# Inference step of a retention and HGRN2 mixer: gates by Silu, loads spaced out, two W_out operands split late

## The chip, the cores and the metric

The program runs on one core of one Trainium2 chip. The metric is the device time of one execution in microseconds. Five engines work side by side: TensorE (PE; its weight loads are listed as PEld), VectorE (DVE), ScalarE (ACT), GpSimd (POOL) and SyncE (SP), which here only issues DMA transfers. Each engine runs its own instructions strictly in its own order and waits at each for what that instruction needs. TensorE's results go to PSUM banks, from which ACT or DVE must copy them before the bank can be used again.

## The reference

One layer for 2048 prompt tokens and 8 decode tokens, width 1024, in fp32. After an RMS norm a projection makes eight groups of 512 columns; a retention branch (4 heads, rotary, fixed decay) and an HGRN2 branch (4 heads, learned forget gate) run over them; each branch's output is normed per head, multiplied by a SiLU gate, and both pass through one output projection.

```python
h = rmsnorm(x, norm_g)
rq, rk, rv, rg, hq, hf, hi, hgate = jnp.split((h @ w_in), 8, axis=-1)
...
o_ret = head_rmsnorm(o_ret, ret_g) * jax.nn.silu(rg)
...
kin = (1.0 - lbf) * jax.nn.sigmoid(-hf)
hq_act = jax.nn.silu(hq)
...
o_hg = head_rmsnorm(o_hg, hg_g) * jax.nn.silu(hgate)
o_cat = jnp.concatenate([o_ret, o_hg], axis=-1)
y = x + o_cat @ w_out
...
y_prompt = rmsnorm(hp, final_norm_g)
```

## The kernel before, in words

**Numbers and products.** A product in fp32 is made of three matmuls: each operand is split into a high part (rounded to the matmul's format, a copy on ACT) and a low part (the rest, a subtraction on DVE). `hi_lo` (L114 to L116) makes that pair; `split` puts it into the pool `wp`, three buffers each for `wh` and `wl`. `three` issues the matmuls (L339). Large products of 256 tokens by 1024 columns are done with seven half-size products instead of eight; this needs sums of the operand's quarters. On the weight side these sums are called T1 to T4, and the quarters used as they are B11, B12, B21, B22 (only B11, B21 and B22 in the seven).

**Stages.**
1. *Projection loop.* Sixteen chunks of 128 tokens form eight token pairs; three sets of weights run over them, so 24 passes, called pairs 0 to 23 here. Set 0 (pairs 0 to 7) makes the two values, set 1 (8 to 15) retention's q and its gate, set 2 (16 to 23) retention's k and HGRN2's gate. Pairs 0 and 1 are done by plain products; for the others `v_pair(i, after)` runs the seven products as steps 0 to 6, about 2.7 us of TensorE each; a product may go on adding in a bank that ACT has just copied (`keep`, L379). `after[n]` lists the side work issued behind step n: loads of the tokens two pairs on (`tok_load`), their scaling, splits and sums one pair on (`tok_ops`, `s_split`), and the sums of squares of the tokens (`stats`, L255 to L265), which give the RMS norm's scale `rs_all`. For pairs 2 to 5 of set 0, `stats(i + 2)` stands behind step 0: four loads of 256 KB into two buffers (`xn`, L262), four Squares on ACT (L263).
2. *The next set's weights.* While set m - 1 runs, pairs j = 3 to 6 of it load two rows of the next set's weights, add the decode tokens' products from them (`wg_decode`), and make the sums T1 to T4 (`w_sums`, L494 to L497), which go to DRAM (`wg_spool`, L520). In pair j = 7 `wg_decode_out` finishes the decode gate (L527 to L532), and `wg_fetch` (L548 to L563) loads the seven operands, 1 MB each: T's through POOL's queue as soon as TensorE has used the old ones, B's through SP. `wg_split` splits them.
3. *Outputs of a pair.* `emit` (L381 to L406) writes what a bank holds: values directly, q and k through the rotation `turn` (L341 to L364, with the table loaded by `rot_load`), gates through Sigmoid on ACT (L399) and a product on DVE (L400).
4. *Retention* rides in set 2 (`r_score`, `r_update`, `r_out`, `r_norm`, `r_turn`); its last chunk, 15, ends in the passage to the scan.
5. *Scan.* Eight units (two halves of the tokens, four HGRN2 heads): projections f and q of a unit run in segments (L980) on TensorE between the levels of the scan of the unit before (L1188 to L1238). Weights for the next projection are brought by `w_load_ahead`. On the side, `t_load_raw`, `t_sum`, `t_spool` and `t_store` make the sums T1 to T4 of W_out, split them and store both parts to DRAM.
6. *Out phase.* Four chunks by plain products (L1572), then six pairs, 2 to 7, by the seven products (`o_pair`); `y_out` norms a chunk and stores it. The last pair, chunks 14 and 15, ends the program.

**Order of the work.** TensorE's order is the order of the program text. The order on ACT, DVE, POOL and SP is laid out at compile time by a scheduler, by the order of the text and by what it reckons each instruction's time to be, with buffers handed out from each pool as they come free. `behind(f)` fixes that what f issues comes after the last instruction issued so far on DVE, ACT and SP; `queued` does so for the engines named. A pool that is opened where another was closed lies on the same storage, so its first use waits for the last use of the old tiles (`scan_pools`, L951 to L958, after `vctx` of the projection loop).

Of the kernel before, what the change touches and what calls it, by code (L numbers as in the profile page):

```python
# [10 lines left out]
F32 = mybir.dt.float32  # L11
# [30 lines left out]
def step_kernel(ctx, tc, a, out):  # L42
# [211 lines left out]

    def stats(i):  # L255
        p = V_ORDER[i]
        ms = sm.tile([P, 4], F32, tag="ms", name=f"ms{p}")
        for j in range(2):
            c = 2 * p + j
            for h in range(2):  # L260
                r = vq.tile([P, GW], F32, tag="xn", name=f"xn{c}{h}", bufs=2)
                sp.dma_start(r, a["x_prompt"][0, c * P : (c + 1) * P, h * GW : (h + 1) * GW])  # L262
                act.activation(r, r, AF.Square, accum_out=ms[:, 2 * h + j : 2 * h + j + 1])  # L263
        pool.tensor_tensor(ms[:, 0:2], ms[:, 0:2], ms[:, 2:4], op=ALU.add)
        rsqrt_mean(rs_all[:, 2 * p : 2 * p + 2], ms[:, 0:2], D, EPS)  # L265
# [106 lines left out]
    def v_pair(i, after):  # L372
# [8 lines left out]
        def emit(c, ty, ps, plus):  # L381
# [15 lines left out]
            if n_set and ty:  # L397
                sg = box[plus] if plus else o
                act.activation(sg, src, AF.Sigmoid)  # L399
                dve.tensor_tensor(o, src, sg, op=ALU.mult)  # L400
# [121 lines left out]
    def wg_decode_out(n):  # L522
# [5 lines left out]
        sg = vq.tile([NB, GW], F32, tag="rg", name=f"gds{n}")  # L528
        act.activation(sg, u, AF.Sigmoid)
        dve.tensor_tensor(u, u, sg, op=ALU.mult)  # L530
# [160 lines left out]
    tok_load(3)  # L691
    dve.tensor_tensor(lbd, lbraw[:, :, 0], lbraw[:, :, 1], op=ALU.subtract)
# [15 lines left out]
    def r_load(c, x):  # L708
        rb_of[c, x] = vq.tile([P, GW], F32, tag="r" + x, name=f"r{x}{c}")
# [75 lines left out]
    def r_steps(p):  # L785
# [22 lines left out]
        if p < N_V:  # L808
# [3 lines left out]
            put(4 + d, lambda: r_load(ca, "g"))  # L812
# [62 lines left out]
    for i in range(2, n_tok):  # L875
# [89 lines left out]
    def seg_steps(w, half, seg, name, evac):  # L965
# [21 lines left out]
    def w_load_ahead():  # L987
        while len(w_ready) < min(w_used[0] + AHEAD, len(want)):
            w_load()
# [281 lines left out]
    def collect(h, u):  # L1271
# [4 lines left out]
        (x, n): dr.tile([P, 2, 4, GW], F32, tag=f"t{x}{n}", name=f"t_dram{x}{n}") for x in "hl" for n in range(2)  # L1276
# [28 lines left out]
    def t_store(k, n):  # L1305
        for x, y in zip("hl", tspl[k, n]):
            sp.dma_start(t_dram[x, n][:, :, k], y.bitcast(F32).rearrange("p (a b) -> p a b", a=2))
# [60 lines left out]
    for k, at in enumerate((0.35, 1.35, 2.35, 4.35)):  # L1368
        steps = [t_load_raw] + [lambda k, n=n: t_sum(k, n) for n in range(4)]
        steps += [lambda k, n=n, f=f: f(k, n) for n in range(2) for f in (t_spool, t_store)]  # L1370
        for f, d in zip(steps, (0, 0.12, 0.18, 0.24, 0.3, 0.4, 0.48, 0.5, 0.58)):
# [154 lines left out]
    def t_load(n, pair):  # L1526
        for x, t in zip("hl", Top[n]):
            sp.dma_start(t.bitcast(F32), t_dram[x, pair[0]][:, pair[1]])

    def t2_load():  # L1530
        for x in "hl":
            t2.append([pools["vp"].tile([P, GW], F32R, tag="v", name=f"oT2{x}{n}") for n in range(4)])
            for n in range(4):
# [333 lines left out]
```

## Time and profile before

| | us |
|---|---|
| median of 3 runs | 1063.98 |
| lowest and highest | 1061.28 and 1064.03 |
| the profiled execution | 1064.47 |
| its span, first to last instruction | 1062.7 |
| its mean granted TensorE clock | 0.993 |

In the page's busy times an engine counts as busy while an instruction runs. A row of the order of time gives the start, the duration, the engine, the line, what is written and read, the count, and in brackets the idle time before it with what ended it. "issue" means that nothing in the profile was waited for. A row of the engine waits gives who waited, for what, the total in us, how often, and the longest. A row of the stretches gives the busy time of each engine, the granted clock of TensorE (1.00 is full speed), the share of the DMA engines that was busy, and GB/s. SPq, ACTq and POOLq mark the issue of a transfer.

### The profile page before, as it was taken

How to read it: one execution, taken by the hardware profiler on the slowest of the kernel's cores; microseconds unless marked ns; L12 is line 12 of the kernel's file. 1: busy time of each engine (PE TensorE's matmuls, PEld its weight loads, DVE VectorE, ACT ScalarE, POOL GpSimd, SP SyncE). 2: the span in 40 equal slices, each digit the busy share in tenths (PEclk: the TensorE clock that was granted, in tenths of full speed). 3: DMA queues.
4: the chain of work that ended last, by engine and by line, in shares of the span. 5: the costliest groups of instructions: out<-in, count | busy, mean ns of one | idle time of the engine just before them, and what ended most of it. 6: DMA issues, size and time to landing. Idle time of an engine off the chain costs nothing. (4 is left out here: it accounts for less than half of the span.)

```text
span 1062.7 us, 21303 instructions
## 1 busy us (share of the span) xinstructions
PE 1037.7 (98%) x8231; PEld 855.2 (80%) x8231; DVE 762.9 (72%) x1404; ACT 548.5 (52%) x1203; POOL 132.9 (13%) x232
## 2 busy tenths in 40 slices
PE   9999999899999999999999999999999999999997
PEld 7778778688787878888888879898778877888775
DVE  6885575887676796676676778777777687668785
ACT  7853343634434755455554656666555474523241
POOL 0410001000000101111111100111021112211122
PEclk9999999999999999999999999999999999999999
DMA  8688899757788855666875696664697366496652
GB/s 293 204 298 306 309 325 320 277 179 271 254 270 256 325 195 172 208 225 219 240 245 176 219 341 237 217 199 164 214 280 230 103 195 197 140 347 206 222 169 99
DMA packets 147462, 248.27 MB, mean 234 GB/s; under 512 B 10944, under 2 KB 78800, under 8 KB 147104
## 3 DMA queue, kind: packets, MB, share of 16 engines
q1 hardware_dynamic: 139632, 221.35, 62.8%
q0 software_dynamic: 7584, 25.29, 6.2%
q8 instruction: 65, 1.06, 0.4%
q14 instruction: 37, 0.30, 0.1%
q10 hardware_dynamic: 144, 0.26, 0.1%
HBM read 162.32 MB, written 84.54 MB: 232 GB/s over the span
## 5 line engine op out<-in xcount | busy, mean ns | idle before, releaser
L1168 ACT ACTIVATE kepth<-kh 128x1024 f32<-128x1024 f32 x24 | 25.4, 1059 | 69.6 <-DVE kh L1158 69.5
L980 PE MATMUL pjfh<-xh,w_h 128*128 128x512 f32 (+2 forms) x160 | 60.2, 376 | 0.0
L980 PE MATMUL pjqh<-xh,w_h 128*128 128x512 f32 (+2 forms) x160 | 60.1, 376 | 0.1
L980 PE MATMUL pjqh<-xh,w_l 128*128 128x512 f32 (+2 forms) x160 | 56.0, 350 | 0.0
L980 PE MATMUL pjfh<-xh,w_l 128*128 128x512 f32 (+2 forms) x160 | 56.0, 350 | 0.0
L980 PE MATMUL pjfh<-xl,w_h 128*128 128x512 f32 (+2 forms) x160 | 56.0, 350 | 0.0
L980 PE MATMUL pjqh<-xl,w_h 128*128 128x512 f32 (+2 forms) x160 | 55.8, 349 | 0.0
L1158 DVE TENSOR_TENSOR kh<-kh,fph 128x512 f32<-128x512 f32 x48 | 33.3, 694 | 20.2 <-PE plh L1188 14.2
L116 DVE TENSOR_TENSOR ab_l<-xr,ab_h 128x512 fp32r<-128x512 f32 (+1 forms) x40 | 37.5, 954 | 4.6 <-ACT ab_h L115 4.4
L752 ACT ACTIVATE obr<-por 128x128 f32<-128x128 f32 x64 | 16.8, 277 | 44.0 <-PE por L739 30.8
L115 ACT ACTIVATE ab_h<-xr 128x512 fp32r<-128x512 f32 (+1 forms) x40 | 32.3, 839 | 13.5 <-DVE xr L293 13.5
L762 DVE SCALAR_TENSOR_TENSOR obr<-por,omr,rg 128x128 f32<-128x128 f32 x64 | 18.0, 344 | 28.9 <-POOL omr L754 28.9
L293 DVE SCALAR_TENSOR_TENSOR xr<-xr,g_in,rb 128x256 f32<-128x256 f32 x64 | 26.7, 479 | 13.1 <-DMA xr<-in_x_t 11.2
L1090 DVE SCALAR_TENSOR_TENSOR obh<-poh,orsh,v 128x128 f32<-128x128 f32 x64 | 18.0, 344 | 25.2 <-POOL orsh L112 25.1
L980 PEld LDWEIGHTS pjqh<-xh,w_h 128*128 128x128 f32 x160 | 30.2, 189 | 5.3 <-issue 1.6
L980 PEld LDWEIGHTS pjfh<-xh,w_l 128*128 128x128 f32 x160 | 30.1, 188 | 4.2
L980 PEld LDWEIGHTS pjqh<-xh,w_l 128*128 128x128 f32 x160 | 30.1, 188 | 4.2
L980 PEld LDWEIGHTS pjfh<-xh,w_h 128*128 128x128 f32 x160 | 30.2, 189 | 3.8
L1161 DVE TENSOR_TENSOR qqh<-qqh,fph 128x512 f32<-128x512 f32 x48 | 32.9, 684 | 0.3 <-ACT kepth L1169 0.3
L980 PEld LDWEIGHTS pjfh<-xl,w_h 128*128 128x128 f32 x160 | 30.3, 189 | 2.7
L980 PEld LDWEIGHTS pjqh<-xl,w_h 128*128 128x128 f32 x160 | 30.2, 189 | 2.7
L1666 DVE SCALAR_TENSOR_TENSOR xro<-xro,yms,fg 128x1024 f32<-128x1024 f32 (+1 forms) x13 | 15.5, 1202 | 19.6 <-POOL yms L112 19.6
(1836 smaller groups left out, 3423.8 us busy)
## 6 DMA issues: line engine op xcount, KB each, us to landing
xr<-a_dram SPq DMA_DIRECT2D x24, 512.0 KB
S<-s_dram SPq DMA_DIRECT2D x24, 512.0 KB
xn<-in_x_prompt SPq DMA_DIRECT2D x32, 256.0 KB
xr<-in_x_t SPq DMA_DIRECT2D x16, 512.0 KB
a_dram<-xr SPq DMA_DIRECT2D x16, 512.0 KB
s_dram<-S SPq DMA_DIRECT2D x16, 512.0 KB
wgr<-in_w SPq DMA_DIRECT2D x16, 512.0 KB
xr<-a_dram SPq DMA_DIRECT2D x32, 256.0 KB
```

The lines of the kernel that those rows point to most:

```text
L115: act.activation(h, src, AF.Copy)
L116: dve.tensor_tensor(l, src, h.bitcast(F32), op=ALU.subtract)
L293: dve.scalar_tensor_tensor(r[:, k], r[:, k], g_in[:, kk : kk + 1], spread_to[i], op0=ALU.mult, op1=ALU.mult)
L752: act.activation(o[:, cc], po[:, h], AF.Square, scale=P ** -0.5, accum_out=ms[:, h : h + 1])
L762: dve.scalar_tensor_tensor(o[:, cc], po[:, h], ms[:, h : h + 1], rb_of[c, "g"][:, cc], op0=ALU.mult, op1=ALU.mult)
L980: pe.matmul(ps, ww[:, kk], x[:, k, b0 : b0 + n], start=(k == 0 and i == 0), stop=(k == KT - 1 and i == 2),)
L1090: dve.scalar_tensor_tensor(ob[g][:, j], po[:, j], rs[:, j : j + 1], gcol(4 * g + j), op0=ALU.mult, op1=ALU.mult)
L1158: dve.tensor_tensor(kv[:, :, 0, :], kv[:, :, 0, :], two[:, :, 1:2].to_broadcast([P, nb, b]), op=ALU.mult)
L1161: dve.tensor_tensor(qv[:, :, 1, :], qv[:, :, 1, :], two[:, :, 0:1].to_broadcast([P, nb, b]), op=ALU.mult)
L1168: act.activation(ss[:, 512:], k[:, :HALF], AF.Copy)
L1666: dve.scalar_tensor_tensor(xro[c][:, cc], xro[c][:, cc], ms[:, 0:1], fg[:, cc], op0=ALU.mult, op1=ALU.mult)
```

## The change

- **Gates.** In `emit` and `wg_decode_out` one Silu replaces Sigmoid and the product on DVE. A one-column Sigmoid is run in the passage to the scan.
- **Token squares.** `stats` is cut into load, sum and end. For pairs 2 to 5, the first half of the loads goes behind step 5 of the pair before (behind the prelude for pair 2), its Squares and the second half's loads behind step 1, the second Squares and the end behind step 4.
- **Rotation.** `rot_load(i + 1)` moves from step 6 to step 4, and the table has two buffers.
- **Gate weights.** Loading, decode products and sums run in pairs j = 2 to 5 of a set instead of 3 to 6; `decode_dg` and `decode_spread`, which scale the decode tokens, move from steps 3 and 5 of pair 2 to steps 0 and 2.
- **Scan weights.** `w_load_ahead` is called at part 2 of a segment too and does one load a call.
- **W_out.** Of the four sums, T1 and T4 are split in the scan as before; T2 and T3 are stored as they are (one store of 512 KB per k), loaded as they are and split in the out phase: T2 in four pieces during the plain chunks, T3 in two pieces behind steps 1 and 2 of pair 2.
- **Chunk 15 of retention.** Its gate is loaded into the pool `rawp`, and `r_norm` runs behind `scan_pools`. The gate of chunk 0 is loaded behind step 6.
- **Last pair.** Chunk 14's final scaling is issued after the last product has been added, ahead of chunk 15's, and is stored through SP instead of POOL.

```diff
+    def stats_load(i, j):
+        c = 2 * V_ORDER[i] + j
+        st[i, j] = [vq.tile([P, GW], F32, tag="xn", name=f"xn{c}{h}", bufs=2) for h in range(2)]
+        for h, r in enumerate(st[i, j]):
+            sp.dma_start(r, a["x_prompt"][0, c * P : (c + 1) * P, h * GW : (h + 1) * GW])
+
+    def stats_sum(i, j):
+        if not j:
+            st[i] = sm.tile([P, 4], F32, tag="ms", name=f"ms{V_ORDER[i]}")
+        for h, r in enumerate(st[i, j]):
+            act.activation(r, r, AF.Square, accum_out=st[i][:, 2 * h + j : 2 * h + j + 1])
...
-        rot[i] = vq.tile([P, 2, P], F32, tag="rot", name=f"rot{i}")
+        rot[i] = vq.tile([P, 2, P], F32, tag="rot", name=f"rot{i}", bufs=2)
...
-                sg = box[plus] if plus else o
-                act.activation(sg, src, AF.Sigmoid)
-                dve.tensor_tensor(o, src, sg, op=ALU.mult)
+                act.activation(o, src, AF.Silu)
...
-        sg = vq.tile([NB, GW], F32, tag="rg", name=f"gds{n}")
-        act.activation(sg, u, AF.Sigmoid)
-        dve.tensor_tensor(u, u, sg, op=ALU.mult)
+        act.activation(u, u, AF.Silu)
...
     tok_load(3)
+    stats_load(4, 0)
...
+        pl, tag = (rawp, "raw") if (c, x) == (2 * N_V - 1, "g") else (vq, "r" + x)
+        rb_of[c, x] = pl.tile([P, GW], F32, tag=tag, name=f"r{x}{c}")
...
-            put(4 + d, lambda: r_load(ca, "g"))
+            put(4 + d if p else 6, lambda: r_load(ca, "g"))
...
-            after[0] += [lambda i=i: stats(i + 2)]
+            after[1] += [lambda i=i: behind(lambda: stats_sum(i + 2, 0)), lambda i=i: stats_load(i + 2, 1)]
+            after[4] += [lambda i=i: behind(lambda: stats_sum(i + 2, 1)), lambda i=i: stats_end(i + 2)]
+            if i + 3 < N_V:
+                after[5] += [lambda i=i: stats_load(i + 3, 0)]
         if N_V <= i + 1 < n_tok:
-            after[6] += [lambda i=i: rot_load(i + 1)]
+            after[4] += [lambda i=i: rot_load(i + 1)]
         if i == 2:
-            after[3] += [decode_dg]
-            after[5] += [decode_spread]
+            after[0] += [decode_dg]
+            after[2] += [decode_spread]
         if m < 3:
-            if 3 <= j < 7:
-                after[0] += [lambda m=m, k=j - 3: wg_load(m, k)]
-                after[4] += [lambda m=m, k=j - 3: wg_decode(m, k), lambda m=m, k=j - 3: wg_spool(m, k)]
+            if 2 <= j < 6:
+                after[0] += [lambda m=m, k=j - 2: wg_load(m, k)]
+                after[4] += [lambda m=m, k=j - 2: wg_decode(m, k), lambda m=m, k=j - 2: wg_spool(m, k)]
...
-                w_load_ahead()
+                w_load_ahead(w_fetch)
+            if part == 2:
+                w_load_ahead(None)
...
-    def w_load_ahead():
-        while len(w_ready) < min(w_used[0] + AHEAD, len(want)):
-            w_load()
+    def w_load_ahead(fetch):
+        n = len(w_ready)
+        if n < min(w_used[0] + AHEAD, len(want)):
+            if fetch is None or n >= 2 * NH:
+                w_load()
+            elif n not in w_raw:
+                fetch()
...
-    def t_spool(k, n):
-        ra, rb, t = traw[k]
-        tspl[k, n] = split((t, ra)[n].rearrange("p a b -> p (a b)"), f"wos{k}{n}")
+    def t_spool(k):
+        tspl[k] = split(traw[k][0].rearrange("p a b -> p (a b)"), f"wos{k}")
...
+    def t_keep(k):
+        sp.dma_start(t_dram["r"][:, :, k], traw[k][2])
...
+                if n == 3:
+                    behind(lambda: act.activation(warm, zero[:, 0:1], AF.Sigmoid))
                 if n == 5:
                     r_last()
-                    r_norm(2 * N_V - 1)
...
             scan_pools()
+            r_norm(2 * N_V - 1)
...
+    def t3_split(n):
+        kk = slice(2 * n, 2 * n + 2)
+        h, l = (t[:, kk] for t in Top["T3"])
+        hi_lo(h, l, l.bitcast(F32))
...
+    def t2_split(n):
+        hi_lo(t2[0][n], t2[1][n], t2[1][n].bitcast(F32))
...
-            ((sp, act)[n] if last else pool).dma_start(out["y_prompt"][0, rows, cc], xro[c][:, cc])
+            ((sp, act)[n] if last else sp if c == T // P - 2 else pool).dma_start(out["y_prompt"][0, rows, cc], xro[c][:, cc])
...
                 if last:
                     y_sq(cb, lo, ms[cb][:, 1:2])
-                    y_out(cb, ms[cb], last)
+                    y_rs(ms[cb])
+                    queued(lambda: y_out(ca, ms[ca], False), (dve,))
+                    queued(lambda: y_out(cb, ms[cb], last), (dve,))
...
+    wd_at[p0] += [(1, lambda: t3_split(0)), (2, lambda: t3_split(1))]
```

More of the change, by code (lines that the diff above doesn't have):

```diff
@@ L253, in slot, with stats_end @@
         return (i - sum(same(n) for n in range(i + 1))) % 2
+    st = {}
+    def stats_load(i, j):
[8 more added lines that the diff above has]
+            act.activation(r, r, AF.Square, accum_out=st[i][:, 2 * h + j : 2 * h + j + 1])
     def stats(i):
-        p = V_ORDER[i]
-        ms = sm.tile([P, 4], F32, tag="ms", name=f"ms{p}")
         for j in range(2):
[L259 to L263, printed above, removed]
+            stats_load(i, j)
+            stats_sum(i, j)
+        stats_end(i)
+    def stats_end(i):
+        p, ms = V_ORDER[i], st[i]
         pool.tensor_tensor(ms[:, 0:2], ms[:, 0:2], ms[:, 2:4], op=ALU.add)
@@ L1275, in step_kernel @@
     t_dram = {
-        (x, n): dr.tile([P, 2, 4, GW], F32, tag=f"t{x}{n}", name=f"t_dram{x}{n}") for x in "hl" for n in range(2)
+        x: dr.tile([P, 2, 4, GW], F32, tag=f"t{x}", name=f"t_dram{x}") for x in "hlr"
     }
@@ L1369, in step_kernel @@
         steps = [t_load_raw] + [lambda k, n=n: t_sum(k, n) for n in range(4)]
-        steps += [lambda k, n=n, f=f: f(k, n) for n in range(2) for f in (t_spool, t_store)]
-        for f, d in zip(steps, (0, 0.12, 0.18, 0.24, 0.3, 0.4, 0.48, 0.5, 0.58)):
+        steps += [t_spool, t_keep, t_store]
+        for f, d in zip(steps, (0, 0.12, 0.18, 0.24, 0.3, 0.4, 0.42, 0.54)):
             side_at.append((at + d, lambda f=f, k=k: f(k)))
@@ L1524, in topv, with t4_load, t3_load @@
         return [t[:, k] for t in Top[op]]
-    def t_load(n, pair):
-        for x, t in zip("hl", Top[n]):
-            sp.dma_start(t.bitcast(F32), t_dram[x, pair[0]][:, pair[1]])
+    def t4_load():
+        for x, t in zip("hl", Top["T4"]):
+            sp.dma_start(t.bitcast(F32), t_dram[x][:, 0])
+    def t3_load():
+        sp.dma_start(Top["T3"][1].bitcast(F32), t_dram["r"][:, 1])
+    def t3_split(n):
+        kk = slice(2 * n, 2 * n + 2)
+        h, l = (t[:, kk] for t in Top["T3"])
+        hi_lo(h, l, l.bitcast(F32))
     def t2_load():
@@ L1703, in o_pair @@
                 y_sq(ca, hi, ms[ca][:, 1:2])
-                y_out(ca, ms[ca], False)
+                y_rs(ms[ca])
+                if not last:
+                    y_out(ca, ms[ca], False)
                 dve.tensor_tensor(xb[:, lo], xb[:, lo], box["u2"], op=ALU.add)
@@ L1735, in step_kernel @@
         (0.8, lambda: op_s34(p0)), (0.85, lambda: op_a(p0)), (0.9, lambda: op_s23(p0)),
-        (0.95, lambda: t_load("T4", (1, 0))),
+        (0.95, t4_load), *((0.76 + 0.06 * n, lambda n=n: behind(lambda: t2_split(n))) for n in range(4)),
     ], key=lambda t: t[0]))
@@ L1754, in step_kernel @@
     op_s14(p0)
-    t_load("T3", (0, 1))
+    t3_load()
     op_a22(p0)
```

21 lines of the change are left out of this document (11 added, 10 removed).

## The prediction

> **What bounds the kernel now.** I read the page first, then who TensorE waited for, then stretches around those waits with the granted clock, and last the order of time on the engine that held TensorE up.
>
> ```profile
> span 1062.7 us, 21303 instructions
> PE 1037.7 (98%) x8231; PEld 855.2 (80%) x8231; DVE 762.9 (72%) x1404; ACT 548.5 (52%) x1203; POOL 132.9 (13%) x232
> ```
>
> TensorE is busy for 1037.7 of 1062.7 us and the change alters no matmul, so all that can be won lies in 25 us of idle TensorE and in stretches where its clock is low. The engine-wait view lists the idle time:
>
> ```profile
> PE pv8a L339 <- ACT s L379: 2.1, 1, 2.1
> PE pkt L716 <- DVE rk L364: 2.1, 1, 2.1
> PE pv4a L339 <- ACT u L379: 1.9, 1, 1.9
> PE plh L1188 <- ACT kepth L1169: 1.5, 1, 1.5
> ...
> PE pv8b L339 <- ACT wv_h L115: 0.9, 1, 0.9
> PE pv8b L339 <- DVE wv_l L116: 0.8, 1, 0.8
> ...
> PE pv16c L339 <- DVE B22l L116: 0.2, 1, 0.2
> ```
>
> Each is one wait in the whole run (columns: total, times, longest). Three of them sit in the projection stage (pairs 4, 8 and 16 of the first loop) and one (plh) at the start of the scan. The stretches right behind three of them, and two more that I need below (columns: stretch, length, busy time of PE, PEld, DVE, ACT, POOL, then clock, DMA share, GB/s):
>
> ```profile
> 61.00:82.00 21.00, 20.89 (x93) 16.90 (x93) 15.52 (x27) 11.73 (x22) 2.05 (x3) 1.00 0.90 294
> 82.00:103.00 21.00, 21.00 (x106) 16.68 (x106) 14.72 (x25) 8.77 (x16) 1.46 (x3) 1.00 0.88 332
> ...
> 168.00:192.00 24.00, 22.33 (x97) 17.64 (x96) 10.04 (x15) 9.91 (x14) 4.57 (x8) 1.00 1.01 355
> ```
>
> ```profile
> 112.50:115.90 3.40, 3.40 (x8) 2.69 (x9) 3.37 (x5) 2.48 (x5) 0.00 (x0) 0.50 0.92 311
> ...
> 194.40:197.80 3.40, 3.12 (x7) 2.51 (x8) 3.40 (x5) 3.40 (x5) 0.00 (x0) 0.50 1.03 412
> ...
> 375.30:378.70 3.40, 3.40 (x10) 2.62 (x9) 3.40 (x4) 2.44 (x6) 0.00 (x0) 0.50 0.70 217
> ```
>
> ```profile
> 600.00:625.00 25.00, 23.18 (x272) 20.80 (x271) 17.11 (x38) 14.86 (x33) 2.81 (x4) 1.00 0.78 266
> ```
>
> After the waits of pairs 4, 8 and 16 the granted clock is 0.50 for 3.4 us, in which 3.4 x 0.5 = 1.7 us of matmul time is lost. So such a wait costs itself and 1.7 us more. The stretch that holds plh's 1.5 us keeps 1.00.
>
> **The change part by part.** The profiled execution took 1064.47 us, 1.77 us beyond its span and 0.49 us above the median of 1063.98; the sum is made against 1064.47 and 0.49 is taken off at the end.
>
> *Token squares spaced, pair 4.*
>
> ```profile
> 102.45 1.88 SPq L262 DMA_DIRECT2D xn<-in_x_prompt  x2
> ...
> 110.01 0.63 ACT L263 ACTIVATE xn<-xn 128x512 f32<-128x512 f32 x1 [4.57 <-DMA xn<-in_x_prompt]
> ...
> 111.77 0.57 ACT L379 ACTIVATE u<-pv4a 128x512 f32<-128x512 f32 x1
> ```
>
> ACT works in order. A Square whose data were issued at 102.45 held it until 110.01, and behind it stood the copy of bank a (u) that TensorE needs before it may add the next product into that bank. The change issues the two halves one step earlier, keeps the second half's load for step 1, and puts the Squares behind the instruction last issued. But the queue ahead of this load is full (spool, 1 MB of xr), and the load moves past only one 256 KB store, 0.77 us at the 332 GB/s of that stretch. Landing at 109.2, two Squares of 0.63 and the copy of 0.57 end at 111.1, where the copy ended at 112.3: 1.2 us of the 1.9 go, about 0.7 stays, and after so short a wait the clock should hold (the 1.5 us wait kept it). I take 1.0 + 1.7 = 2.7 us. Bounds: 0 (the load lands as late as now) to 1.9 + 1.7 = 3.6. The same moves in pairs 2, 3 and 5 hide under their matmuls, as now.
>
> *Rotation loads at step 4 with two buffers, pair 16.*
>
> ```profile
> 367.57 0.68 DVE L394 TENSOR_TENSOR rk<-pv16b,s 128x512 f32<-128x512 f32 x1
> 371.61 0.69 DVE L359 TENSOR_TENSOR t<-rk,rot 128x512 f32<-128x512 f32 x1 [3.36 <-DMA rot<-in_rot]
> ...
> 373.01 0.69 DVE L364 TENSOR_TENSOR rk<-t,t 128x512 f32<-128x512 f32 x1
> 373.62 1.22 DVE L116 TENSOR_TENSOR B22l<-wg2B,B22h 128x1024 fp32r<-128x1024 f32 x1
> ```
>
> DVE stood 3.36 us for a 128 KB table; rk was ready at 368.25. The turn takes 373.70 - 371.61 = 2.1, so with the table there it ends at 370.4, before TensorE asks (373.7 - 2.1 = 371.6). B22l, next on DVE, then ends at 371.6 instead of 374.8, so its 0.2 us goes too. 2.1 + 0.2 + 1.7 = 4.0, of which I take 3.9; bounds 2.0 (B22 or T4 late by a microsecond, clock still lost) to 4.0. This is the surest term.
>
> *Gate weights one pair sooner, and Silu, pair 8.*
>
> ```profile
> 171.87 0.77 ACT L527 ACTIVATE gd<-pgd 8x256 f32<-8x256 f32 x2 [2.85 <-DMA v_dram<-vo]
> 172.66 0.63 ACT L529 ACTIVATE gds<-gd 8x512 f32<-8x512 f32 x1
> ...
> 174.04 0.31 SPq L532 DMA_DIRECT2D dg_dram<-gd  x1
> ...
> 175.21 3.08 SPq L562 DMA_DIRECT2D wg1B<-in_w  x4
> ...
> 185.23 1.06 ACT L115 ACTIVATE wv_h<-wg1B 128x1024 fp32r<-128x1024 f32 x1 [5.39 <-DMA wg1B<-in_w]
> ...
> 188.82 1.06 ACT L115 ACTIVATE wv_h<-wg1B 128x1024 fp32r<-128x1024 f32 x1 [2.53 <-DMA wg1B<-in_w]
> ```
>
> ```profile
> L89 ACT ACT_TABLE_LOAD  x1: 1283/1283/1283, 0.7 to 0.7; - x1
> ```
>
> ```profile
> L400 DVE TENSOR_TENSOR vo<-vo,u x17: 681/684/691, 212.4 to 585.9; 128x512 f32<-128x512 f32 x17
> L400 DVE TENSOR_TENSOR vo<-vo,p x15: 681/692/694, 207.4 to 549.9; 128x512 f32<-128x512 f32 x15
> ```
>
> The second half of B21 landed at 188.8 and TensorE lost 0.9 + 0.8 + 2.1 = 3.8 us, plus 1.7 of clock. The DMA share is 1.01 there: seven 1 MB operands are fetched within one pair. The change takes a pair's 1 MB load and 1 MB spool out of pair 6, so the queue is empty when the fetch starts and the store that gd waited 2.85 us for lands about a microsecond earlier. Against it: B21's load stands on SP behind the store of gd, which stands behind the first Silu. The trace has one table load, for the Sigmoid at the start, so I reckon with a second at this place (1.28) and save DVE's product (0.7): 0.6 us later. Net 0.4 us earlier for SP, and some 0.6 from a shorter queue: +1.0, clock still lost. Bounds: -2.0 (the whole table load and no shorter queue) to 3.8 + 1.7 = 5.5. That the fetch alone fills the DMA engines is why I stay near the bottom. By the Trainium skill (ScalarE: Activation LUTs, What ACT_TABLE_LOAD costs) such a switch is about 1283 ns of load, as the row has it, and about 1380 ns of drain, which no run here shows; with it this term would be -0.4 and the forecast 1056.9.
>
> The 32 products that Silu removes (17 x 0.684 + 15 x 0.692 = 22 us of DVE) lie under matmuls in stretches where DVE is 70% busy: nothing. If that cover were gone it would be 0.7 us a gate. The load of Sigmoid's table for the scan comes with the warm-up in an idle stretch of ACT (4.1 us of it before 599.45, below): nothing; uncovered 1.3.
>
> *The price in pair 2.* 2 MB more in a stretch of 21 us is 95 GB/s on top of 294, at a share of 0.90 already. The backlog, (294 + 95) / 294 x 0.90 = 1.19, is 4 us of queue. A token pair's loads are wanted a pair later, so mostly hidden; I take -0.8, bounds 0 to -3.8 (one wait of 2.1 and its clock). decode_dg and decode_spread move ahead with it, unchanged, since the sums need xs: nothing.
>
> *Start of the scan: T2 and T3 unsplit, last norm later, weights sooner.*
>
> ```profile
> 599.45 0.28 ACT L752 ACTIVATE obr<-por 128x128 f32<-128x128 f32 x1 [4.10 <-issue]
> ...
> 603.99 0.60 ACT L1023 ACTIVATE fsh<-pjfh 128x512 f32<-128x512 f32 x1 [3.39 <-issue]
> ...
> 611.81 1.06 ACT L115 ACTIVATE wos00h<-wot 128x1024 fp32r<-128x1024 f32 x1 [1.26 <-DVE wot L1295]
> ...
> 618.84 1.06 ACT L115 ACTIVATE w_h<-wr 128x1024 fp32r<-128x1024 f32 x1 [3.24 <-DMA t_dramh<-wos00h]
> ```
>
> ACT idles 3.39 us before the scan's first Sigmoid because its tile lies on storage of the first loop, freed only by the last norm; that norm now reads a gate in other storage. And w_h waited 3.24 us for the store of a W_out split to free a buffer; half of these splits go. Both lead to plh's 1.5 us; with the small waits around it I take +2.0, bounds 0.5 to 2.2. w_load still fetches and splits in one call, half a 512-segment sooner: nothing, its buffer being the limit. t_keep writes 512 KB in place of 1 MB.
>
> *Out phase and tail.* T2 costs four splits of 512 columns and T3 two of 1024, by the rows of that size 2 x (1.06 ACT + 1.22 DVE) and again as much for T2: they replace four in the scan. T3's fall in this stretch (columns as above), where TensorE never waits and DVE is busy for 12.8 of 20 us: nothing. Uncovered it would be 4 x 1.22 = 4.9.
>
> ```profile
> 935.00:955.00 20.00, 20.00 (x89) 16.26 (x88) 12.82 (x20) 6.28 (x12) 2.48 (x7) 1.00 0.94 357
> ```
>
> ```profile
> 1052.62 1.29 DVE L1666 SCALAR_TENSOR_TENSOR xro<-xro,yms,fg 128x1024 f32<-128x1024 f32 x1 [2.05 <-POOL yms L112]
> ...
> 1055.21 0.69 DVE L1714 TENSOR_TENSOR xro<-xro,po 128x512 f32<-128x512 f32 x1
> 1057.89 1.41 DVE L1666 SCALAR_TENSOR_TENSOR xro<-xro,yms,fg 128x512 f32<-128x512 f32 x2 [1.99 <-POOL yms L112]
> ```
>
> TensorE's last product lets DVE start at 1055.21, so the tail is 1062.7 - 1055.2 = 7.5 us. The 1.29 us for chunk 14 move from 1052.62 into DVE's gap of 1.99 behind 1055.90: hidden. But its 512 KB leave on SP ahead of the final 256 KB: -0.3, bounds 0 to -1.5 (512 KB at 357 GB/s, all in front).
>
> **Sum:** 2.7 + 3.9 + 1.0 - 0.8 + 2.0 - 0.3 = 8.5; 1064.47 - 8.5 = 1056.0, less 0.49: **1055.5 us**.
>
> The Trainium skill (TensorE: Matmul & The Clock Gate, HAM oscillation) asks for idle gaps above about 3.4 us before the clock falls. The rows disagree: waits of 1.9 and 2.1 us were followed by 0.50. By that rule the two refunds of 1.7 would not be there, and the time 1058.9.
>
> **The rivals.** *Fetch in time:* pair 8 runs clear, because with pair 6 free everything lands 5 us earlier. For it: the share of 1.01; against: the fetch itself makes it. Pair 8 gives 5.5 instead of 1.0: 1051.0.
>
> *Waits only move:* pair 4 keeps its wait and pair 8 loses 2.0, by its lower bound; 3.9 + 2.0 - 2.0 - 0.8 - 0.3 = 2.8: 1061.2. For it: ACT in order stays, and six loads still share a full queue.
>
> *Slower, the load queue fills from pair 2 on:* the backlog of 4 us is carried, since 0.88 in pair 3 leaves 2.5 us a pair to work it off; a Square then blocks ACT in pairs 2, 3, 4 and 5 as it does in 4 now. 4 x 3.8 = 15.2 against 3.6 now is a loss of 11.6; with 3.9 + 1.0 + 2.0 - 0.3 = 6.6 gained: 1064.47 + 5.0 - 0.49 = 1069. It decides when a Square's data land more than about 7.5 us after issue (110.0 - 102.45 now). Against it: loads issued at step 5 have nearly two steps more before their Square.
>
> *A table load at each alternation:* the last eight pairs mix Square and Silu, 16 groups of each; if they share no table, up to 32 x 1.28 = 41 us of ACT; a quarter of it reaching TensorE gives 10.3: 1065.8. Against it: Square ran beside Sigmoid with one load in the run. The Trainium skill (ScalarE: Activation LUTs, Table sets) counts cheap functions as filler of every set, but does not name Square.
>
> **How the numbers follow.** Forecast (1052 to 1060) 0.55; fetch in time 0.13; waits move 0.13; slower 0.13; table loads 0.04; the rest elsewhere. The range, 1049 to 1064, leaves out the slower case, half the table case and the extreme of the first rival. Faster means below 1060.8 (0.3%, about what this measurement can tell): 0.55 + 0.13 + 0.05 of the moving waits = 0.73. Slower, above 1067.2: 0.14. Within: 0.13.
>
> **What would show it.** Right: no wait of pkt on rk and no 0.50 clock near 375; pv4a waiting under 1 us; two more table loads, one before pair 8 and one near 595; fsh starting within 1 us of the last Square of chunk 15; DVE busy near 740. Wrong: a wait in pairs 2 or 3 behind a Square, pv8b waiting longer than 1.7 us, a tail above 8 us, or waits of TensorE after 935 us.

## The result, and the profile after

| | before | after |
|---|---|---|
| median, us | 1063.78 (4 runs) | 1050.37 (4 runs) |
| lowest and highest | 1061.28 and 1064.03 | 1047.95 and 1051.37 |
| profiled execution / its span | 1064.47 / 1062.7 | 1047.95 / 1046.2 |

The ratio is 0.9876, 95% interval [0.9853, 0.9899]: 13.4 us less between the medians. The profiled execution of after is the fastest of its four, so the two traces lie 16.5 us apart. The forecast was 1055.5.

The page of after, with the same columns as before:

```profile
span 1046.2 us, 21268 instructions
...
PE 1029.7 (98%) x8231; PEld 851.1 (81%) x8231; DVE 742.4 (71%) x1372; ACT 552.6 (53%) x1208; POOL 130.9 (13%) x231
```

TensorE runs the same 8231 matmuls in 8.0 us less busy time, of which the three stretches at half clock make 3 x 1.7 = 5.1, and stands idle 16.5 us in place of 25.0. No stretch of after before its last matmul has a clock below 1.00. Its waits, by the view of the engine waits:

```profile
PE plh L1208 <- DVE Abh L1214: 1.5, 1, 1.5
...
PE pv3a L352 <- ACT vo L409: 1.1, 1, 1.1
...
PE pgd L592 <- DMA wgr<-in_w: 0.8, 2, 0.6
```

The waits of pv4a, pkt, pv8a, pv8b and of plh on kepth are gone. New are small ones in pairs 3 (pv3a) and 5 (pgd). To see where 16.5 us went, I took the length of each pair from the start of its first matmul to that of the next pair's. For pair 8 these are the first starts in the rows of the banks pv8a and pv9a, here after, then before:

```profile
L352 PE MATMUL pv8a<-wv_h,ab_h x4: 389/389/389, 182.1 to 184.2; 128*128 128x512 f32 x4
...
L352 PE MATMUL pv9a<-wv_h,ab_h x4: 389/391/398, 202.2 to 204.3; 128*128 128x512 f32 x4
```

```profile
L339 PE MATMUL pv8a<-wv_h,ab_h x4: 389/390/390, 184.5 to 186.5; 128*128 128x512 f32 x4
...
L339 PE MATMUL pv9a<-wv_h,ab_h x4: 389/391/397, 211.0 to 213.0; 128*128 128x512 f32 x4
```

So pair 8 fell from 26.5 to 20.1 us. All places with a difference, by this reading:

| place | before | after | gain | forecast |
|---|---|---|---|---|
| start of the run and pairs 2 and 3 | | | -2.0 | -0.8 |
| pair 4 | 24.5 | 20.8 | 3.8 | 2.7 |
| pair 5 | 21.2 | 21.8 | -0.7 | 0 |
| pair 6 | 20.8 | 19.5 | 1.2 | 0 |
| pair 8 | 26.5 | 20.1 | 6.4 | 1.0 |
| pairs 10 and 14 | | | 0.0 | 0 |
| pair 16 to its first par | 22.2 | 17.9 | 4.2 | 3.9 |
| pair 19 | 29.7 | 30.1 | -0.4 | 0 |
| scan, first pjfh to first py | 282.2 | 278.6 | 3.6 | 2.0 |
| last matmul to the end | 7.5 | 7.3 | 0.2 | -0.3 |
| sum, before rounding | | | 16.5 | 8.5 |

1.2 us of pair 2's loss and pair 6's gain are the same decode matmuls, moved; pairs 10 and 14 exchange as much again.

The stretches of pair 8 in after (busy times, clock, DMA share, GB/s):

```profile
184.00:192.00 8.00, 8.00 (x37) 6.64 (x36) 5.95 (x6) 6.04 (x7) 0.00 (x0) 1.00 1.03 414
192.00:195.40 3.40, 3.40 (x17) 2.81 (x16) 3.37 (x6) 2.16 (x3) 0.00 (x0) 1.00 0.52 207
```

The DMA engines are as full as before, share 1.03, and yet TensorE works all 8.00 us. What changed is when the operand it needs next has landed. The order of time on SP and on ACT in pair 7 of after:

```profile
158.28 0.43 SPq L571 DMA_DIRECT2D wg1B<-in_w  x1
...
165.29 1.79 SPq L571 DMA_DIRECT2D wg1B<-in_w  x3
170.05 0.31 SPq L541 DMA_DIRECT2D dg_dram<-gd  x1
```

```profile
168.10 1.28 ACT L539 ACT_TABLE_LOAD   x1
169.40 0.63 ACT L539 ACTIVATE gd<-gd 8x512 f32<-8x512 f32 x1
...
174.64 2.00 ACT L115 ACTIVATE wv_h<-wg1B 128x1024 fp32r<-128x1024 f32 x2
...
177.37 2.00 ACT L115 ACTIVATE wv_h<-wg1B 128x1024 fp32r<-128x1024 f32 x2
```

Four halves (B11 and B21) are issued before the store of gd, not behind it, and ACT splits both halves of B21 from 177.37 on with no wait; before, the second waited until 188.82. ACT's order also changed in pair 4:

```profile
109.80 0.60 ACT L392 ACTIVATE u<-pv4a 128x512 f32<-128x512 f32 x1 [2.38 <-PE pv4a L352]
...
113.07 0.62 ACT L267 ACTIVATE xn<-xn 128x512 f32<-128x512 f32 x1
```

The copy u of bank a runs as soon as TensorE has filled it; the Square stands behind it, where before it stood ahead and held it. These orders are laid out at compile time, so each of them could come from any edit. That is what the experiments had to sort out.

### The profile page after: what moved, and what is told of

The parts are those of the page before. It is cut to its first block, busy times and chain, and to the rows that moved or that the text cites. A ratio compares the mean times of both kernels' runs of the same rounds, so it can differ in the third digit from the quotient of the medians.

```text
span 1046.2 us, 21268 instructions
## 1 busy us (share of the span) xinstructions
PE 1029.7 (98%) x8231; PEld 851.1 (81%) x8231; DVE 742.4 (71%) x1372; ACT 552.6 (53%) x1208; POOL 130.9 (13%) x231
## 3 DMA queue, kind: packets, MB, share of 16 engines
q8 instruction: 65, 1.06, 0.4%
## 4 chain that ended last, share of the span: by engine, by line
PE 86%; DMA 4%; ACT 4%; DVE 4%; issue 1%; POOL 0%; SPq 0%; DVEq 0%; POOLq 0%; ACTq 0%
PE po L352 11%; PE pjfh L996 9%; PE pjqh L996 8%; PE py L1607 4%; PE plh L1208 2%; DMA xn<-in_x_prompt 1%; PE par L735 1%; PE puh L1083 1%; PE poh L1099 1%; PE pur L742 1%; PE por L748 1%; PE por L750 1%; PE poh L1101 1%; PE pv21a L352 1%; PE pv20a L352 1%
## 5 line engine op out<-in xcount | busy, mean ns | idle before, releaser
L411 ACT ACTIVATE vo<-vo 128x512 f32<-128x512 f32 x32 | 20.1, 630 | 27.1 <-DVE vo L405 12.3
L996 PEld LDWEIGHTS pjqh<-xh,w_h 128*128 128x128 f32 x160 | 30.1, 188 | 5.0 <-issue 1.6
L996 PEld LDWEIGHTS pjfh<-xh,w_l 128*128 128x128 f32 x160 | 30.1, 188 | 4.2
L996 PEld LDWEIGHTS pjqh<-xh,w_l 128*128 128x128 f32 x160 | 30.1, 188 | 4.2
```

The lines of the kernel that those rows point to most:

```text
L411: act.activation(o, src, AF.Silu)
L996: pe.matmul(ps, ww[:, kk], x[:, k, b0 : b0 + n], start=(k == 0 and i == 0), stop=(k == KT - 1 and i == 2),)
```

## The experiments

Medians of runs on two chips are compared by their ratio to the kernel before, run beside them.

**1. The gate sums alone, and all the rest without them.** In the kernel before, the first edit; in the one after, its reverse:

```diff
-            if 3 <= j < 7:
-                after[0] += [lambda m=m, k=j - 3: wg_load(m, k)]
+            if 2 <= j < 6:
+                after[0] += [lambda m=m, k=j - 2: wg_load(m, k)]
```

> The kernel before with only the gate weight sums one pair sooner (and the decode tokens' scaling ahead of them). Theory: pair 8 takes about 20 to 21 us instead of 26.5, pairs 2 and 5 gain about 1.5 us of waits: 1063.8 - 6.4 + 1.5 = about 1059. Rival (it takes Silu or the spaced loads as well): pair 8 keeps at least 4 us of its waits, 1063 or more. The forecast's slower case (a queue that fills from pair 2 on, with the old unspaced squares): waits of 2 us and lost clock in two or more of pairs 2 to 5, 1066 or more.

> The changed kernel with the gate weight sums back in pairs 3 to 6. Theory (these sums decide pair 8): pair 8, from its first matmul to pair 9's, takes about 26 us again instead of 20.1, with 0.50 of the clock behind it, while pairs 2 and 5 lose the 1.5 us of new waits: 1050.4 + 6.4 - 1.5 = about 1055. Rival (Silu or the spaced loads cleared pair 8): pair 8 stays at about 20 us, and the time falls to about 1049.

| | median | ratio and interval | pair 4 | pair 8 | pair 16 | scan |
|---|---|---|---|---|---|---|
| after | 1050.37 | 0.9876 [0.9853, 0.9899] | 20.8 | 20.1 | 17.9 | 278.6 |
| gate sums alone | 1054.54 | 0.9917 [0.9901, 0.9933] | 20.8 | 20.1 | 18.7 | 282.0 |
| gate sums late | 1057.09 | 0.9928 [0.9905, 0.9951] | 22.0 | 28.8 | 17.9 | 278.6 |

The gate sums one pair sooner clear pair 8 by themselves, and without them it is slow again: 28.8 us, 2.3 more than before, of which 1.7 are a second stretch at half clock. They clear pair 4 and most of pair 16 too, which the expectation had not counted, though squares and rotation stand there as before. ACT in pair 4 of the kernel with the gate sums alone:

```profile
110.44 0.60 ACT L379 ACTIVATE u<-pv4a 128x512 f32<-128x512 f32 x1 [2.38 <-PE pv4a L339]
...
113.71 0.62 ACT L263 ACTIVATE xn<-xn 128x512 f32<-128x512 f32 x1
```

The unspaced Square has gone behind u here as well: the compile-time order was laid out anew. The scan keeps its 282 us, so its gain comes from the scan's own edits.

The other way round, the rest of the change without the gate sums shortens pair 4 from 24.5 to 22.0 us and pair 16 from 22.2 to 17.9. In that kernel a Square does stay ahead of u, only its data land sooner, and TensorE waits 0.9 us with no stretch at half clock behind it:

```profile
108.45 0.63 ACT L267 ACTIVATE xn<-xn 128x512 f32<-128x512 f32 x1 [3.56 <-DMA xn<-in_x_prompt]
...
110.22 0.57 ACT L392 ACTIVATE u<-pv4a 128x512 f32<-128x512 f32 x1
```

```profile
PE pv4a L352 <- ACT u L392: 0.9, 1, 0.9
```

So pairs 4 and 16 have two cures, either of which does most of the work, and their gains do not add up.

**2. Amount or order?** The gate sums change two things for B21: 2 MB less traffic in pair 6, and, through the new order, B21's loads ahead of the store of gd. Three kernels take these apart. In after, B21's loads are pinned behind the store:

```diff
-                    after[n] = [lambda m=m, op=op: wg_fetch(m, op)] + after[n]
+                    tie = behind if (m, op) == (1, "B21") else lambda f: f()
+                    after[n] = [lambda m=m, op=op, t=tie: t(lambda: wg_fetch(m, op))] + after[n]
```

> The changed kernel with one thing pinned: the two loads of B21 for pair 8 stand behind the store of the decode gate on SP, as they did before; the data moved in each pair are the same. Theory A (the place on SP decides): B21 lands late again, pair 8 takes 23 to 26 us instead of 20.1, 1053 to 1057. Theory B (it is the 2 MB taken out of pair 6 that count): pair 8 stays within 0.7 us of 20.1, 1050 to 1051.

In before, the decode gate with its store goes behind step 2 of pair 7:

```diff
-                after[0] += [lambda m=m: wg_decode_out(m)]
+                after[0 if m == 2 else 2] += [lambda m=m: wg_decode_out(m)]
```

> The kernel before with one thing moved: the decode gate of set 1 is finished behind step 2 of pair 7 instead of step 0, so that its store stands behind B21's loads on SP; the sums stay in pairs 3 to 6. Theory A (place on SP): pair 8 loses most of its 6.4 us of waits and clock, 1057 to 1060. Theory B (amount): pair 8 stays above 25 us, 1063 to 1065.

In after, pair 6 gets its traffic back:

```diff
+            if i == 6:
+                after[0] += [lambda: wg_load(1, 0)]
+                after[4] += [lambda: wg_back(1, 0)]
```

> The changed kernel with one thing added in pair 6 of the first loop: the 1 MB load that stood there before (the same slabs of another pair's weights once more) and 1 MB of stores to a scratch tensor that nobody reads; no arithmetic on any engine. Theory (the 2 MB that left pair 6 are what cleared pair 8): pair 8 lasts 25 to 29 us in place of 20.1, waits for the halves of B21 with a stretch at half clock, and the time is 1055.5 to 1057.5. Rival (what cleared it is the work of VectorE, GpSimd and TensorE that left pair 6, or the order of the instructions): pair 8 stays below 22 us and the time at 1050.4 within 1.5.

The row to read is ACT's split of B21's second half, against the start of pair 8. It stands at 188.82 before (quoted in the prediction), and in the pinned kernel, the one with the store moved, and the refilled one at:

```profile
183.31 1.06 ACT L115 ACTIVATE wv_h<-wg1B 128x1024 fp32r<-128x1024 f32 x1 [3.36 <-DMA wg1B<-in_w]
```

```profile
184.62 1.06 ACT L115 ACTIVATE wv_h<-wg1B 128x1024 fp32r<-128x1024 f32 x1 [2.71 <-DMA wg1B<-in_w]
```

```profile
186.08 1.06 ACT L116 ACTIVATE wv_h<-wg1B 128x1024 fp32r<-128x1024 f32 x1 [2.60 <-DMA wg1B<-in_w]
```

| B21's second half, us after the start of pair 8 | B21 behind the store | B21 ahead of it |
|---|---|---|
| 2 MB in pair 6 | +4.3 (before), +4.0 (refilled) | -0.2 (store moved) |
| pair 6 empty | +1.1 (pinned) | -3.8 (after) |

The figures are starts of ACT's split. In the other three kernels it waited for the data; in after it did not, so there the data landed at -3.8 or sooner. The second half is the later one of the row at 177.37, about 0.95 us in. (The kernel with the gate sums alone has one half ahead of the store and one right behind it, and reaches -3.8 too.) Each of the two changes is worth 3 to 5 us of landing, or more in the steps that end at after, and they add up. TensorE begins B21's products 2.7 us into the pair, those of the second half 1.4 later, and the split takes 1.06 on ACT and 1.2 on DVE, so that at +1.1 little is late and at -0.2 nothing should be. In time this gives:

| | median | ratio and interval | pair 8 |
|---|---|---|---|
| pinned behind the store | 1050.32 | 0.9875 [0.9853, 0.9897] | 22.3 |
| store moved (before otherwise) | 1061.57 | 0.9981 [0.9967, 0.9996] | 24.8 |
| pair 6 refilled | 1054.99 | 0.9914 [0.9885, 0.9942] | 24.7 |

With pair 6 empty the order is worth nothing in the median; the pinned kernel's trace, its slowest run, shows a wait of 1.4 us, for the copy s of bank a, which stands on ACT behind the splits that B21 held up. Refilling pair 6 without any arithmetic brings back 4.6 us of pair 8 (just under the 25 us expected, and with no stretch at half clock there), though the work that left pair 6 did not come back. But the refill also put B21 back behind the store, as SP's rows show, and its runs scatter from 1049.08 to 1056.86; like with like, the traffic alone is 24.7 against the 22.3 of the pinned kernel, 2.4 us:

```profile
170.82 0.30 SPq L546 DMA_DIRECT2D dg_dram<-gd  x1
...
171.62 2.34 SPq L576 DMA_DIRECT2D wg1B<-in_w  x4
```

The store moved helps less than its -0.2 promises, and the rows of DVE say why:

```profile
183.71 0.68 DVE L359 TENSOR_TENSOR t0d<-gd,rotd 8x512 f32<-8x512 f32 x1 [2.79 <-DMA rotd<-in_rotd]
...
184.99 1.20 DVE L116 TENSOR_TENSOR wv_l<-wg1B,wv_h 128x1024 fp32r<-128x1024 f32 x1
```

The decode gate's rotation moved along with its store; DVE waited 2.79 us for an 8-row table, and the low part of B11 stood behind it. TensorE waited 2.8 us for that. One wait had taken another's place.

**3. The spacing, given the gate sums.** Squares as one block behind step 0, rotation at step 6 with one buffer, in after.

```diff
-            after[1] += [lambda i=i: behind(lambda: stats_sum(i + 2, 0)), lambda i=i: stats_load(i + 2, 1)]
...
+            after[0] += [lambda i=i: stats(i + 2)]
...
-            after[4] += [lambda i=i: rot_load(i + 1)]
+            after[6] += [lambda i=i: rot_load(i + 1)]
```

> The changed kernel with two parts undone: the token squares are issued together as before, and the rotation tables have one buffer and are loaded at step 6. Theory (the gate sums one pair sooner already clear pairs 4 and 16, as they did alone): the time stays at 1050.4 within 1.5 us; pair 4 lasts 21 to 22 us and pair 16 up to the end of its last matmul about 18.7, with no stretch at half clock. Rival (the spacing does what the prediction says of it): pair 4 waits for a bank copy again for 1 to 1.9 us and pair 16 for the rotation for about 2, each with 1.7 us of clock: 1050.4 + 2.7 + 3.9 = 1057.0.

1052.02, ratio 0.9896 [0.9881, 0.9911]; pair 4 is 20.8 us as in after, pair 16 is 19.8 in place of 17.9. The squares' spacing shows nothing; the rotation's is worth 1.9 us, most of it TensorE's wait for the turned k, as DVE waits for the table:

```profile
PE pkt L726 <- DVE rk L377: 1.2, 1, 1.2
```

```profile
361.93 0.69 DVE L372 TENSOR_TENSOR t<-rk,rot 128x512 f32<-128x512 f32 x1 [4.02 <-DMA rot<-in_rot]
```

Neither expectation held whole: the rotation does matter, but without the half clock that followed the longer wait before.

**4. The parts of the scan.** In after, T2 and T3 split and stored in the scan again; the last norm back at its place in the last pair; the weight load in one call again.

```diff
-        steps += [t_spool, t_keep, t_store]
+        steps += [lambda k, n=n, f=f: f(k, n) for n in range(2) for f in (t_spool, t_store)]
```

> The changed kernel with the two W_out sums split in the scan and stored as pairs, as before. Theory (the splits held the w_h copies by their stores): the scan, 278.6 us from its first projection to the first output product, grows by 2 to 3.5 us, the start's wait of plh comes back with 1 to 1.5 us, the time is 1052.4 to 1053.9, and nothing is gained in the out phase. Rival (the last norm's place gives the scan's 3.4 us): the scan stays at 278.6 and the time at 1050.4. Second rival (the splits moved to the out phase cost something there): the out phase is shorter and the time below 1050.

```diff
                     r_last()
+                    r_norm(2 * N_V - 1)
...
             scan_pools()
-            r_norm(2 * N_V - 1)
```

> The changed kernel with the norm and gate of the last chunk at their old place in the out of the last pair, its gate's data in the first loop's storage. Theory (a minor share of the scan's gain): the first Sigmoid of the scan starts about 3 us later behind the last Square, the scan grows by 0 to 1.4 us, the time is 1050.4 to 1051.8. Rival (it gives all of it): the scan grows by 3.4 us and the time is 1053.8.

```diff
-                w_load_ahead(w_fetch)
-            if part == 2:
-                w_load_ahead(None)
+                w_load_ahead()
```

> The changed kernel with the scan's weight load in one call at the first step of a half segment, as before. Theory (nothing, as the prediction has it): the scan stays at 278.6 us from its first projection to the first output product within 0.4, the time at 1050.4. Rival (the earlier fetch is the part of the scan's gain that the splits and the last norm leave): the scan grows by 0.5 to 1.5 us and the time is 1051 to 1052.

| in after, undone | median | ratio and interval | scan |
|---|---|---|---|
| W_out splits | 1051.52 | 0.9891 [0.9876, 0.9905] | 281.1 |
| last norm | 1050.59 | 0.9886 [0.9869, 0.9902] | 280.2 |
| weight load | 1049.24 | 0.9867 [0.9846, 0.9889] | 278.6 |

The splits are worth 2.6 us of the scan and the last norm 1.6 (4.2 together, 0.6 more than both give: they overlap), the weight load nothing. The totals agree in sign, but each ratio lies inside the interval of after's, so the sizes rest on the traces. The split's row on ACT and TensorE's waits with the splits back, then ACT's first Sigmoid and TensorE's waits with the norm back:

```profile
604.98 1.06 ACT L115 ACTIVATE w_h<-wr 128x1024 fp32r<-128x1024 f32 x1 [2.27 <-DMA t_dramh<-wos00h]
```

```profile
PE plh L1208 <- ACT kepth L1189: 1.4, 2, 1.0
...
PE poth L1117 <- DVE obh L1110: 0.4, 1, 0.4
```

```profile
591.60 0.60 ACT L1043 ACTIVATE fsh<-pjfh 128x512 f32<-128x512 f32 x1 [3.39 <-issue]
```

```profile
PE pjqh L996 <- ACT fxh L1044: 0.7, 1, 0.7
...
PE pah L1226 <- DVE fph L1169: 0.4, 1, 0.4
```

None of these four waits stands in after. The 3.39 us are the same idle time as in the kernel before, and in after they are gone:

```profile
582.76 1.28 ACT L1529 ACT_TABLE_LOAD   x1
...
587.31 0.22 ACT L763 ACTIVATION_READ_ACCUMULATOR obr<-por 128x1 f32 x1
587.40 0.61 ACT L1043 ACTIVATE fsh<-pjfh 128x512 f32<-128x512 f32 x1
```

**5. Gates by Sigmoid again.**

```diff
-                act.activation(o, src, AF.Silu)
+                act.activation(sg, src, AF.Sigmoid)
+                dve.tensor_tensor(o, src, sg, op=ALU.mult)
```

> The changed kernel with each gate as Sigmoid and a product again. Theory (the products lie under matmuls): VectorE is busy for about 22 us more (764), the table loads fall to one, the time is 1050.4 within 1.5 us. Rival (the products delay banks and splits in the pairs where VectorE is 70% busy): some five waits of 0.7 us, 1053.9. Second rival (the table loads cost their 1.28 us each): 1047.8.

1049.83, ratio 0.9872 [0.9857, 0.9887], with 20.9 us more on DVE (742.4 in after):

```profile
PE 1030.9 (98%) x8231; PEld 851.3 (81%) x8231; DVE 763.3 (73%) x1406; ACT 550.3 (53%) x1206; POOL 130.8 (12%) x231
```

The Silu moves nothing that can be measured.

**6. The last pair.** Chunk 14's output at its old place and on GpSimd's queue.

```diff
-            ((sp, act)[n] if last else sp if c == T // P - 2 else pool).dma_start(out["y_prompt"][0, rows, cc], xro[c][:, cc])
+            ((sp, act)[n] if last else pool).dma_start(out["y_prompt"][0, rows, cc], xro[c][:, cc])
```

> The changed kernel with the output of chunk 14 back at its old place on VectorE and on GpSimd's queue. Prediction's step (the tail gains 0.3 by the new order): the time from TensorE's last product to the end, 7.3 us, becomes 7.6. Theory from the trace of after (7.52 before, 7.32 after: the edit is worth 0.2): 7.5. Rival (the 512 KB on SP ahead of the last store cost more than the order gains): 7.0 or less. The time stays at 1050.4 within 1 us in each.

(The prediction had the new order cost 0.3, not gain it, as this expectation misquotes.) 1050.05, ratio 0.9874 [0.9849, 0.9899]. From the last matmul to the end it took 8.4 us, as no theory had it, because DVE stood 1.3 us behind TensorE in the last pair of that run. From the start of DVE's last sum (1041.97) to the end (1049.04) it is 7.1 us, against 7.3 in after and 7.5 before. DVE's rows with the old order, then of after:

```profile
1041.97 0.69 DVE L1753 TENSOR_TENSOR xro<-xro,po 128x512 f32<-128x512 f32 x1
1044.64 1.41 DVE L1703 SCALAR_TENSOR_TENSOR xro<-xro,yms,fg 128x512 f32<-128x512 f32 x2 [1.99 <-POOL yms L112]
```

```profile
1038.92 0.69 DVE L1754 TENSOR_TENSOR xro<-xro,po 128x512 f32<-128x512 f32 x1 [1.43 <-PE po L352]
1039.52 1.28 DVE L1703 SCALAR_TENSOR_TENSOR xro<-xro,yms,fg 128x1024 f32<-128x1024 f32 x1
1041.78 1.42 DVE L1703 SCALAR_TENSOR_TENSOR xro<-xro,yms,fg 128x512 f32<-128x512 f32 x2 [0.99 <-POOL yms L112]
```

The 1.28 us fall into the wait for yms as predicted, and 0.99 of it is left. Whether the edit gains anything stays open: tenths of a microsecond.

**7. An attempt to do better.** Pair 5's new wait on wgr comes from a load issued at 128.3 and needed at 136. Its decode products go one step later.

```diff
-                after[4] += [lambda m=m, k=j - 2: wg_decode(m, k), ...
+                after[5 if j == 5 else 4] += [lambda m=m, k=j - 2: wg_decode(m, k), ...
```

> The changed kernel with one more edit: the decode products with the gate weights, and the sums' stores, stand at step 5 in place of 4 in pair 5 (and 13), so that the 1 MB load, which lands at 137 and for which TensorE waits 1.0 us, has a step more. Theory: that wait goes, pair 5 is 0.6 to 1.0 us shorter, the stores are out before pair 8's fetch begins: 1049.4 to 1049.8. Rival (the stores one step later meet the fetch, or the order on SP that this changes sends B21 behind the gate store): pair 8 longer by 1 us or more, the time 1050.4 to 1052.

1049.35, ratio 0.9869 [0.9847, 0.9892]. The wait is gone and pair 5 is 20.8 us, but pair 8 is 21.7, with two waits of 0.5 for bank copies. No gain can be told from the interval.

## Why the prediction came out 5 us high

The measured 1050.37 lies within the range given (1049 to 1064), near its lower end, and outside the forecast's own 1052 to 1060.

**Pair 8 is the term that was mis-sized:** 1.0 forecast, 6.4 measured, and it had its bounds too low as well (5.5). The bound adds up the waits listed and the clock; the 0.9 us beyond it lie in matmuls beside those waits, which in before begin up to 0.40 us after the one ahead where the steady distance is 0.23. Two steps failed. "That the fetch alone fills the DMA engines is why I stay near the bottom": they are full in after too (1.03), but what decides is when B21 lands, and without pair 6's traffic it lands about 3 us earlier even behind the store (+4.3 to +1.1), where the step reckoned 0.6 for a shorter queue. "B21's load stands on SP behind the store of gd" was read from the order before; the new order, laid out at compile time, put the loads ahead, another 4.9 us or more (+1.1 to -3.8). In pair 8 itself less traffic alone gave 4.2 us of the 6.4 (26.5 to 22.3, pinned); the order alone gave 1.7 (to 24.8), because the wait for the table rotd took the place of the old one. The rival "fetch in time" had the traffic right, at 1051.0, and got a chance of 0.13.

**Pairs 4 and 16** came out near their sizes (3.8 for 2.7, 4.2 for 3.9). The waits and their clock were right, and so was what the spacing does by itself: with the gate sums late pair 4 gains 2.5 for the 2.7 forecast, by the step forecast, a Square ahead of u whose data come sooner, with 0.9 us of waiting left for the 0.7 forecast; pair 16 gains 4.3. In the whole change another cause came first. The gate sums by themselves clear pair 4 and leave pair 16 only 0.8 us behind after, and with them in place the spacing is worth 0 and 1.9: ACT's order was laid out anew, and no Square stands ahead of u. That these two terms fit the total is in part luck, since the forecast gave the gate sums no share in them.

**The price** was larger than forecast: 0.8 in pair 2 and 3 beyond the moved matmuls, 0.7 in pair 5, 0.4 in pair 19 (a wait for obr that came and went from kernel to kernel). I put its being small down to the reason given, that a pair's loads are wanted a pair later; no run tests that. The slower rival's condition, a Square whose late data hold ACT in pairs 2 to 5, is not met in the trace of after. But one of the signs of being wrong, a wait in pair 2 or 3 behind a Square, is there in small. TensorE ends with bank pv2a at 78.96; the copy vo begins at 79.41, behind two Squares, which makes 0.4 of the 1.1 us of pv3a (0.7 with the squares unspaced):

```profile
78.80 0.61 ACT L267 ACTIVATE xn<-xn 128x512 f32<-128x512 f32 x1
...
79.41 0.57 ACT L409 ACTIVATE vo<-pv2a 128x512 f32<-128x512 f32 x1
```

**The scan** gave 3.6 for 2.0, above its bound of 2.2, since the norm's 1.6 and the splits' 2.6 add up nearly; the bound had been taken from TensorE's waits at the scan's start. There an ACT that starts 3.4 us late costs 0.7 us for fxh and 0.4 for fph even without plh's wait, and 0.9 of the 3.6 us were won 190 us further on, around poth, which waits 0.3 us in before and 0.4 with the splits back. The weight load is worth nothing, as forecast. The **out phase** is unchanged (T2 and T3 cost TensorE no wait there), and the **tail** gave 0.2 where it was to cost 0.3.

**Silu** is worth nothing either way, and DVE is busy 742.4 us, as expected near 740. Two more table loads came, 1.28 us each, at 168.10 and 582.76. The Trainium skill (ScalarE: Activation LUTs, What ACT_TABLE_LOAD costs) adds some 1380 ns of drain to each. Here ACT's last copy ends at 168.08, the load starts at 168.10 and the Silu at 169.40, so nothing of a drain shows and the forecast's 1.28 was the right price. The alternation of Square and Silu loads no table.

## What to carry to other kernels

A full transfer queue can be relieved ahead of the rush: taking 2 MB out of the pair before the rush brought B21 3 us forward, though the rush itself stayed as dense. When a wait is traced to "operand landed late", write down what it would take to land in time, from the queue's content and from the issue order separately, before settling on a share of it. And where the order of an engine is laid out by a scheduler, an edit in one place can rearrange another: run each edit alone, and the whole without it, since the squares' spacing in pair 4 was worth nothing with the gate sums in place and, with the other edits, 2.5 us without them.

## What was not expected of the hardware

Whether the half clock follows a wait depends on where the wait falls. In the fourteen profiles of this study, eight waits of TensorE in the projection loop were 1.9 to 2.8 us long; six were followed by a granted clock near 0.50 for 3.4 to 7 us, two were not. In the refilled kernel the 2.1 us of pv8a is one of these two, while 1.6 us for potr in pair 19 was followed by the low clock:

```profile
PE pv8a L353 <- ACT s L393: 2.1, 1, 2.1
PE potr L786 <- DVE obr L778: 1.6, 1, 1.6
```

No other wait below 1.9 us before the kernel's last matmul was followed by it. The low stretches keep to a grid of 3.413 us. In the trace of before they start at 112.49, 194.41, 375.32 and 1057.98 us, which is 24, 53 and 200 such steps apart; those of the three other kernels that have more than one lie whole steps apart as well, and the long one of 6.83 us with the gate sums late lasts two steps. Here are the step that holds pv4a's wait in before and the one behind it, then steps of the refilled kernel, two that share pv8a's wait and the one behind, and that of potr with the one behind:

```profile
109.08:112.49 3.41, 1.51 (x8) 0.94 (x6) 2.41 (x7) 2.41 (x7) 0.00 (x0) 1.00 0.88 336
112.49:115.90 3.41, 3.41 (x8) 2.70 (x9) 3.38 (x5) 2.50 (x5) 0.00 (x0) 0.50 0.92 311
```

```profile
186.88:190.29 3.41, 1.92 (x6) 1.05 (x6) 3.12 (x4) 3.41 (x5) 0.00 (x0) 1.00 1.04 414
190.29:193.70 3.41, 1.76 (x8) 1.45 (x9) 3.41 (x4) 3.41 (x6) 0.00 (x0) 1.00 1.04 413
193.70:197.12 3.42, 3.42 (x17) 2.82 (x16) 3.42 (x6) 2.46 (x4) 0.00 (x0) 1.00 0.95 383
...
436.11:439.52 3.41, 1.82 (x9) 1.03 (x8) 3.41 (x12) 0.36 (x1) 0.00 (x0) 1.00 0.31 100
439.52:442.93 3.41, 3.41 (x11) 2.72 (x11) 1.35 (x2) 1.32 (x5) 0.80 (x1) 0.50 0.66 184
```

Before the last matmul there are seven low stretches. In the step ahead of six of them TensorE was busy for 0.73 to 1.51 us, and no whole step of the fourteen profiles up to the last matmul had so little work and kept the full clock (the least was 1.54, around pkt's wait with the store moved). Potr's step with 1.82 is the exception, so the busy time is not the whole measure; that stays open. Where the steps lie against the program differs between profiles: the low stretch of pair 4 starts at 112.49 in before and at 113.62 with the store moved, and these are not whole steps apart.

The Trainium skill (TensorE: Matmul & The Clock Gate, HAM oscillation) names gaps above about 3.4 us. Every low stretch here before the last matmul came behind shorter ones, so the rule does not hold for this kernel, and a refund of 1.7 us behind a wait of 2 us is likely, not certain.
